# A two-layer encoder trunk on one core: how the MLPs' up products are placed, who adds the weight blocks, and when weights are loaded

## The chip, the cores and the metric

The kernel runs on one core of a Trainium2 chip. The metric is the device time of one execution in microseconds; the kernel before has a median of 1085.5 us over three runs (1084.59 to 1086.11).

## The reference

The input is 512 tokens of width 1024, float32. Two layers, each a token mixer and an MLP, with an RMSNorm ahead of each and residual adds:

```python
for layer in range(DEPTH):                       # DEPTH = 2
    hn = rmsnorm(h, norm_mix[layer])
    mix = chunked_band_attention(...) if layer == 0 else rglru_block(...)
    h = h + mix
    h = h + sq_relu_mlp(rmsnorm(h, norm_mlp[layer]), mlp_w1[layer], mlp_w2[layer])
return rmsnorm(h, norm_final)

def sq_relu_mlp(h, w1, w2):                      # w1: 1024 x 4096, w2: 4096 x 1024
    z = jax.nn.relu(h @ w1)
    return (z * z) @ w2
```

The change touches the two MLPs alone.

## The kernel before

**Split operands.** Each float32 operand is cast to a rounded part H (ScalarE, L156) and the rest L = raw − H (VectorE, L159), and each product is three matmuls, H·H, H·L and L·H (`mm3`, L253 to L256). So every weight tile of 128x1024 costs a ScalarE cast and a VectorE subtraction before TensorE can use it. `plan` lists the weight tiles in the order of their use; `want(n)` hands out the next n and lets `fetch` prepare tiles up to three ahead. The H and L buffers are five each (`wsp`), so a tile is cast when the buffer of the fifth before it is free.

**The MLP.** The hidden width of 4096 is cut into four parts p of 1024. The *up* products make the hidden values of a part, Relu and Square on ScalarE follow, and the *down* products of the part are added into the result tile `d`. Part 0's up products are eight plain tiles of 512 columns (`up`). All other products are done on blocks of a 2x2 partition with seven products in place of eight (Strassen–Winograd):

- An up *group* (p, g), with g = 0 or 1, makes half a part: seven *pieces* of 24 matmuls of 256 columns. Pieces use the weight tiles u11, us2, u12, us1, us3, us4, u22 in this order, and the activations hn or the sums r1 to r4. They accumulate in the PSUM banks b1, b6 and b5. Three partial results are kept: `c1`, a copy of b1 after the first piece (L777), `u` and `v`, VectorE sums of b6 and b5 with c1 (L782, L790). `out_` adds what is missing on VectorE (L769) and does Relu and Square (L771, L772).
- A down *round* p has seven *steps*, each 24 matmuls of 512 columns over two token tiles: weights 11, t1, 22, 21, t2, t3, t4 (two half tiles each) against the split hidden blocks 11, s1, s4, 12, s2, s3, 22. They accumulate in the PSUM bank pairs X and Y. After each step `read` (L723, VectorE) adds two banks into `d`, scaled by the norm's factor. `split` (L808, L809) splits the hidden blocks, `sums` and the subtraction at L850, L820, L821 and L816 form s1 to s4.

**Weight sums.** The block sums us1 to us4 and t1 to t4 are made by *adding transfers*: DMAs from the POOL queue with `accum_op=add`, onto a block in SBUF from HBM or from SBUF. us1 is the block 21 loaded into `kept` plus 22 (L124), us2 a second copy of 11 plus us1 (L125), us3 is 11 plus 21 (L170), us4 is 12 plus us2 (L172). Of a round's t blocks, t1 is 12 plus 11 from HBM (L116), t3 is 22 reloaded into 11's buffer plus 12 (L163, L164), t2 is 22 plus 12 (L166), t4 is 21 plus t2 (L168). SP's queue issues all plain loads; a group's loads are issued when its first tile is fetched (`upper`, L119 to L125), a round's when its tile 11 is fetched (`blocks`).

**Order.** In part 0's eight up products, `turn` moves the residual into `d`: 16 transposes on VectorE and 32 DMAs of 64 KB on SP (L716), and r1 to r4 are formed. In round p the first group of part p+1 is interleaved one piece behind each step; the second group of part p (for p > 0) runs before or within the opening of round p, five or six pieces in a row. Each engine runs its instructions in an order that the build fixes; it follows the order of the code where data and buffers are ready and moves ready instructions forward.

Of the kernel before, what the change touches and what calls it, by code (L numbers as in the profile page):

```python
# [40 lines left out]
def trunk(ctx: ExitStack, tc: tile.TileContext, xT, cols, gfin, win, wqkv, wo, rwin, rga, rgx, rwo, w1, w2, out):  # L41
# [59 lines left out]
    raws, start_ = {}, []  # L101

    def rows(src, h):
        return src[h * U : (h + 1) * U].rearrange("(k p) c -> p k c", p=P)
# [4 lines left out]
    def blocks(srcs):  # L109
        for name, src in srcs.items():  # L110
            both = state["raw"].tile([P, 2, 1024], F32, name=f"b{name}_{state['next']}", tag=f"b{name}")
            for h in range(2):
                raws[name, h] = both[:, h]
                nc.sync.dma_start(two(raws[name, h]), rows(src, h))
        for h in range(2):
            G.dma_start(two(raws["12", h]), rows(srcs["11"], h), accum_op=ALU.add)  # L116

    def upper(srcs):
        i = state["next"]  # L119
        for n, tag, src in (("11", "wr0", "11"), ("s1", 0, "21"), ("s2", "wr1", "11"), ("12", "wr2", "12"), ("22", 1, "22")):  # L120
            raws["u" + n] = state["kept"][:, tag] if n in ("s1", "22") else wraw.tile([P, 1024], F32, name=f"u{n}_{i}", tag=tag)
            nc.sync.dma_start(raws["u" + n].rearrange("p (k c) -> p k c", k=4), srcs[src].rearrange("(k p) c -> p k c", p=P))
        raws["us3"], raws["us4"] = raws["u11"], raws["u12"]
        G.dma_start(raws["us1"].rearrange("p (k c) -> p k c", k=4), srcs["22"].rearrange("(k p) c -> p k c", p=P), accum_op=ALU.add)  # L124
        G.dma_start(raws["us2"], raws["us1"], accum_op=ALU.add)  # L125

    def fetch():
        i = state["next"]
        kind, nk, srcs = plan[i]
        H = wsp.tile([P, 1024], F32R, name=f"wh{i}", tag="wh")  # L130
        L = wsp.tile([P, 1024], F32R, name=f"wl{i}", tag="wl")
        n = 1024
        if kind == "plain":
            n = nk * sum(src.shape[1] for src in srcs)
# [4 lines left out]
            for n_, src in enumerate(srcs):  # L139
                w = src.shape[1]  # L140
                queue = nc.scalar if i == 0 and n_ else nc.sync
                queue.dma_start(rv[:, :, c0 : c0 + w], src.rearrange("(k p) c -> p k c", p=P))
                c0 += w
        elif kind[0] == "u":
            nk = 4
            if kind == "u11":
                upper(srcs)
            raw = raws[kind]
        else:
            half, nk = nk, 2  # L150
            if kind == "11" and half == 0:
                blocks(srcs)
            raw = raws[{"t1": "12", "t2": "22", "t3": "11", "t4": "21"}.get(kind, kind), half]
        state["next"] += 1
# [7 lines left out]
        if kind == "11":  # L162
            nc.sync.dma_start(two(raw), rows(srcs["22"], half))  # L163
            G.dma_start(two(raw), rows(srcs["12"], half), accum_op=ALU.add)  # L164
        elif kind == "22":
            G.dma_start(raw, raws["12", half], accum_op=ALU.add)  # L166
        elif kind == "21":
            G.dma_start(raw, raws["22", half], accum_op=ALU.add)  # L168
        elif kind == "u11":
            G.dma_start(raw.rearrange("p (k c) -> p k c", k=4), srcs["21"].rearrange("(k p) c -> p k c", p=P), accum_op=ALU.add)  # L170
        elif kind == "u12":
            G.dma_start(raw, raws["us2"], accum_op=ALU.add)  # L172
# [31 lines left out]
    starts = []  # L204

    def add_mlp(layer):
        starts.append(len(plan))
        def up_(p, j):
            c0 = 2 * p * T + j * P
            plan.append(("plain", KT, [w1[layer][:, c0 : c0 + P]]))  # L210

        def add_group(p, g):
            c0 = (2 * p + g) * T
            srcs = {
# [3 lines left out]
            plan.extend(("u" + n, 4, srcs) for n in ("11", "s2", "12", "s1", "s3", "s4", "22"))  # L218

        for j in range(KT):  # L220
            up_(0, j)
        for p in range(4):
            srcs = {
# [3 lines left out]
            if p:  # L227
                add_group(p, 1)
            tail = [plan.pop()] if p == 3 else []
            if p < 3:  # L230
                add_group(p + 1, 0)
                tail = plan[-7:]
                del plan[-7:]
            for kind in ("11", "t1", "22", "21", "t2", "t3", "t4"):
                plan.extend((kind, half, srcs) for half in range(2))
                plan.extend(tail[:1])
                del tail[:1]
# [409 lines left out]
    def mlp(ly, norm):  # L647
        with ExitStack() as mctx:
# [23 lines left out]
            def right_split(n):  # L672
# [6 lines left out]
                if n == 4:  # L679
                    state["kept"] = per.tile([P, 2, 1024], F32, name=f"kept{ly}", tag="hx1")  # L680
# [47 lines left out]
            def up(p, j):  # L728
# [11 lines left out]
                if 1 <= j <= 2:  # L740
                    for k in range(4 * j - 4, 4 * j):
                        scaled(k)
                if 3 <= j <= 6:
                    for step_, n in (((right, 1), (right, 3)), ((right, 2), (right, 4), (right_split, 1)),
                                     ((right_split, 3),), ((right_split, 2), (right_split, 4)))[j - 3]:
                        step_(n)
# [10 lines left out]
            def group(p, g):  # L757
# [19 lines left out]
                S.copy(c1, b1)  # L777
# [11 lines left out]
                v = zp.tile([P, T], F32, name=f"v{ly}{p}{g}", tag="v")  # L789
                V.tensor_add(v, b5, c1)  # L790
# [8 lines left out]
                out_(1, 0, b6, c1, -1.0)  # L799
                yield  # L800

            def round_(p):
                low, raw = {}, {}
                raw["11"], raw["s1"] = a[p, 0, 0], a[p, 0, 1]

                def split(n, h):
                    H, L = zp.tile([P, 4, U], F32R, name=f"{h}{n}{ly}{p}", tag=h), take(F32R, f"l{n}{p}")
                    S.copy(H, raw[n])  # L808
                    V.tensor_sub(L, raw[n], f(H))  # L809
                    low[n] = (H, L)  # L810
                    give(raw[n])

                def sums(last):
                    if last:
                        raw["s4"] = take(F32, f"s4{p}")
                        V.scalar_tensor_tensor(raw["s4"], raw["12"], -1.0, raw["s2"], ALU.mult, ALU.subtract)  # L816
                    else:
                        raw["12"], raw["22"] = a[p, 1, 0], a[p, 1, 1]
                        raw["s2"] = take(F32, f"s2{p}")
                        V.tensor_sub(raw["s1"], raw["22"], raw["s1"])  # L820
# [39 lines left out]
                else:  # L860
# [3 lines left out]
                    for n in range(5):  # L864
                        next(here)
# [351 lines left out]
```

## Time and profile before

| what | value |
|---|---|
| median of 3 runs | 1085.5 us |
| profiled execution, its own time | 1087.62 us |
| its span (first to last instruction) | 1085.8 us |
| mean granted TensorE clock | 0.982 |
| TensorE busy | 1035.0 us, 95% |
| VectorE busy | 832.3 us, 77% |
| ScalarE busy | 638.5 us, 59% |
| first MLP: first up matmul to last down matmul | 244.7 us to 589.2 us |
| second MLP: first up matmul to the end of the span | 733.6 us to 1085.8 us |

Times inside the profile count from the start of the span. A row of the table of stretches gives, for a stretch of time, the busy time of each engine with its number of instructions, the granted clock of TensorE (1.00 is full), the busy share of the DMA engines (overlapping packets can carry it over 1) and GB/s. A row of the timeline gives start, length, engine, line, operation, `out<-in` by the program's tile names, and in brackets how long the engine stood idle before it and what ended that. Rows of waits give the total, the number and the longest.

### The profile page before, as it was taken

What the parts mean: (1) busy time and instruction counts of PE and PEld (TensorE: products, weight loads), DVE (VectorE), ACT (ScalarE), POOL (GpSimd) and SP (SyncE); (2) the same over time, 40 slices, a digit from 0 to 9 for tenths busy, and PEclk for the clock granted to TensorE, in tenths of its full rate; (3) what the DMA queues carried; (4) which work ended last, traced back from release to release, by engine and by line L of the source; (5) the groups of instructions that cost most, each with busy time, mean ns of one, the idle gap of its engine ahead of it and who ended that gap; (6) DMA issues with size and microseconds to landing.
All of it is one profiled execution on the core that took longest, in us unless ns stands there. A gap on an engine that the chain in (4) does not pass through costs nothing. (4 is left out here: it accounts for less than half of the span.)

```text
span 1085.8 us, 15138 instructions
## 1 busy us (share of the span) xinstructions
PE 1035.0 (95%) x5618; PEld 896.1 (83%) x5618; DVE 832.3 (77%) x1212; ACT 638.5 (59%) x984; POOL 129.1 (12%) x140
## 2 busy tenths in 40 slices
PE   9999999999959799999999999999959799999997
PEld 8788888888848798998978788888848798998976
DVE  7889778877458597787798998976447487697686
ACT  7667567457535465565567697556535365565565
POOL 1000000000121122122110000000221122121120
PEclk9999999999979999999999999999979899999999
DMA  8354253343979899999863313354969899999772
GB/s 272 99 145 127 59 175 97 93 150 89 284 135 277 216 193 247 274 198 261 242 117 101 113 59 97 96 175 118 290 108 274 219 184 236 282 202 254 184 152 78
DMA packets 149098, 189.27 MB, mean 174 GB/s; under 512 B 7585, under 2 KB 105889, under 8 KB 149025
## 3 DMA queue, kind: packets, MB, share of 16 engines
q1 hardware_dynamic: 119008, 128.87, 37.4%
q0 software_dynamic: 29440, 58.73, 31.2%
q8 instruction: 44, 0.72, 0.3%
q10 hardware_dynamic: 576, 0.72, 0.2%
q14 instruction: 30, 0.24, 0.1%
HBM read 148.43 MB, written 2.10 MB: 139 GB/s over the span
## 5 line engine op out<-in xcount | busy, mean ns | idle before, releaser
L156 ACT CAST wh<-b 128x1024 fp32r<-128x1024 f32 x112 | 117.0, 1049 | 77.9 <-PE m L255 53.1
L159 DVE TENSOR_TENSOR wl<-b,wh 128x1024 fp32r<-128x1024 f32 x112 | 135.7, 1221 | 16.1 <-ACT wh L156 16.0
L254 PE MATMUL m<-rH,wh 128*128 128x256 f32 x384 | 110.2, 287 | 22.4 <-ACT wh L156 22.4
L256 PE MATMUL m<-rH,wl 128*128 128x256 f32 x384 | 110.1, 287 | 2.3 <-DVE wl L159 2.3
L255 PE MATMUL m<-rL,wh 128*128 128x256 f32 x384 | 109.7, 286 | 0.0
L159 DVE TENSOR_TENSOR wl<-wr,wh 128x1024 fp32r<-128x1024 f32 (+1 forms) x74 | 87.7, 1189 | 17.5 <-ACT wh L156 17.0
L156 ACT CAST wh<-wr 128x1024 fp32r<-128x1024 f32 (+1 forms) x73 | 75.0, 1030 | 43.9 <-PE wo L255 11.8
L254 PEld LDWEIGHTS m<-rH,wh 128*128 128x128 f32 x384 | 74.8, 195 | 24.3 <-ACT wh L156 23.4
L254 PE MATMUL m<-hnH,wh 128*128 128x256 f32 x288 | 83.7, 291 | 11.6 <-ACT c L777 11.6
L159 DVE TENSOR_TENSOR wl<-u,wh 128x1024 fp32r<-128x1024 f32 x48 | 58.7, 1224 | 38.6 <-ACT wh L156 38.1
L255 PE MATMUL m<-hnL,wh 128*128 128x256 f32 x288 | 83.2, 289 | 0.0
L256 PE MATMUL m<-hnH,wl 128*128 128x256 f32 x288 | 83.1, 289 | 0.0
L156 ACT CAST wh<-u 128x1024 fp32r<-128x1024 f32 x48 | 50.4, 1049 | 53.1 <-PE x L256 19.3
L256 PEld LDWEIGHTS m<-rH,wl 128*128 128x128 f32 x384 | 74.7, 194 | 3.3 <-DVE wl L159 3.3
L255 PEld LDWEIGHTS m<-rL,wh 128*128 128x128 f32 x384 | 74.9, 195 | 0.9
L254 PEld LDWEIGHTS m<-hnH,wh 128*128 128x128 f32 x288 | 56.9, 198 | 13.1 <-ACT c L777 12.3
L116 POOL DMA_DIRECT2D b<-in_w x16 | 22.9, 1464 | 365.2 <-DMA b<-in_w 364.6
L159 DVE TENSOR_TENSOR wl<-us,wh 128x1024 fp32r<-128x1024 f32 x12 | 14.7, 1222 | 62.5 <-ACT wh L156 62.5
L255 PEld LDWEIGHTS m<-hnL,wh 128*128 128x128 f32 x288 | 56.9, 198 | 0.7
L256 PEld LDWEIGHTS m<-hnH,wl 128*128 128x128 f32 x288 | 56.9, 198 | 0.0
L156 ACT CAST wh<-us 128x1024 fp32r<-128x1024 f32 x12 | 12.6, 1046 | 73.1 <-DMA us<-kept 56.7
L256 PE MATMUL y<-wh,ls 128*128 128x512 f32 x128 | 50.2, 392 | 1.4 <-DVE ls L809 1.4
(383 smaller groups left out, 3077.1 us busy)
## 6 DMA issues: line engine op xcount, KB each, us to landing
b<-in_w SPq DMA_DIRECT2D x80, 512.0 KB, 8.1
b<-in_w POOLq DMA_DIRECT2D x32, 512.0 KB, 7.5
b<-b POOLq DMA_DIRECT2D x32, 512.0 KB, 7.0
u<-in_w SPq DMA_DIRECT2D x24, 512.0 KB, 10.0
kept<-in_w SPq DMA_DIRECT2D x24, 512.0 KB, 8.9
wr<-in_wqkv SPq DMA_DIRECT2D x20, 512.0 KB, 4.0
wr<-in_w SPq DMA_DIRECT2D x16, 512.0 KB, 4.2
wr<-in_rwin SPq DMA_DIRECT2D x16, 512.0 KB, 3.7
```

The lines of the kernel that those rows point to most:

```text
L116: G.dma_start(two(raws["12", h]), rows(srcs["11"], h), accum_op=ALU.add)
L156: S.copy(H[:, :n], raw[:, :n])
L159: low = V.tensor_sub(L[:, :n], raw[:, :n], f(H[:, :n]))
L254: PE.matmul(acc, WH, XH, start=start, stop=False, skip_group_check=more)
L255: PE.matmul(acc, WH, XL, start=False, stop=False, skip_group_check=more)
L256: PE.matmul(acc, WL, XH, start=False, stop=stop, skip_group_check=more)
```

## The change

**Order.** The eight up products of part 0 are traced ahead of round 0 (before, the last four stood inside it). In rounds 0 to 2 all 14 pieces of both groups of part p+1 are interleaved, two behind each step (behind the last step one, `sums`, one, `sums`). Round 3 has no pieces. `opening` and `sums` of the next round are done at the end of the round before it.

**Who adds weight blocks.** us2, us4 and both halves of t2 and t3 are now made on VectorE (an add or a subtraction of 128x1024 in SBUF, in `fetch`). us1, us3, t1 and t4 stay adding transfers; t1 and t4 add from SBUF. The second load of 11 in a group and the reload of 22 in a round go.

**Copies inside PSUM.** Where b1 was copied to `c1` and later added by VectorE, ScalarE copies b1 into b6, and piece r2 accumulates onto it (`piece(b6, "r2", False)`). `u` and `v` become ScalarE copies of b6 and b5. In a round X is copied into Y after step s4 and step 12 accumulates onto it; step 11 is no longer read.

**Loads.** A block is loaded as soon as its buffer's last use is fetched, one block at a time, for the group or round that follows; for the first ones the calls stand in `up` (j = 1, 3, 5) and behind the last plain tile.

```diff
+    def load_down(key, name): ...      # two SP loads of a block of the next round
+    def first_sum(key):
+        if key in down:
             for h in range(2):
-        for h in range(2):
-            G.dma_start(two(raws["12", h]), rows(srcs["11"], h), accum_op=ALU.add)
+                G.dma_start(raws["12", h], raws["11", h], accum_op=ALU.add)
+    def load_up(key, name):
...
+        raws["u" + name] = raw
+        nc.sync.dma_start(four(raw), rows(upper[key]["21" if name == "s1" else name]))
+        if name == "s1":
+            G.dma_start(four(raw), rows(upper[key]["22"]), accum_op=ALU.add)
...
             nk = 4
-            if kind == "u11":
-                upper(srcs)
+            following = (key[0], key[1] + 1)
+            if kind == "us2":
+                raws["us2"] = wraw.tile([P, 1024], F32, name=f"us2_{key[0]}{key[1]}", tag=f"wr{(state['base'] + 2) % 3}")
+                V.tensor_add(raws["us2"], raws["u11"], raws["us1"])
+                raws["us3"] = raws["u11"]
+                G.dma_start(four(raws["us3"]), rows(upper[key]["21"]), accum_op=ALU.add)
+            if kind == "us4":
+                raws["us4"] = raws["u12"]
+                V.tensor_add(raws["us4"], raws["us4"], raws["us2"])
             raw = raws[kind]
...
+            if kind == "t2":
+                V.tensor_add(raw, raw, raws["12", half])
+                G.dma_start(raws["21", half], raw, accum_op=ALU.add)
+            if kind == "t3":
+                V.tensor_sub(raw, raws["22", half], raw)
...
+        if kind == "plain_":
+            state["base"] = state["plain"] % 3
+            load_up((nk_layer[i], 0), "11")
+            load_up((nk_layer[i], 0), "12")
+        elif kind == "us1":
+            load_up(following, "s1")
+        elif kind == "us3":
+            load_up(following, "11")
+        elif kind == "us4":
+            load_up(following, "12")
+        elif kind == "u22":
+            load_up(following, "22")
+        elif kind == "t2" and half:
+            load_down(following, "12")
+        elif kind == "t3" and half:
+            load_down(following, "11")
+            first_sum(following)
+        elif kind == "t4" and half:
+            load_down(following, "22")
+            load_down(following, "21")
...
+            ups = [("u" + n, 4, (layer, 2 * p + g)) for g in range(2) for n in ("11", "s2", "12", "s1", "s3", "s4", "22")]
+            for n, kind in enumerate(("11", "t1", "22", "21", "t2", "t3", "t4")):
+                plan.extend((kind, half, (layer, p)) for half in range(2))
+                if p < 3:
+                    plan.extend(ups[2 * n : 2 * n + 2])
...
-                b1 = mmp(f"m1{ly}{p}{g}")
+                b1, b6 = mmp(f"m1{ly}{p}{g}"), mmp(f"m6{ly}{p}{g}")
                 piece(b1, "11", True)
-                c1 = wk.tile([P, T], F32, name=f"c1{ly}{p}{g}", tag="nsq", bufs=2)
-                S.copy(c1, b1)
+                S.copy(b6, b1)
                 yield
-                b6 = mmp(f"m6{ly}{p}{g}")
-                piece(b6, "r2", True)
+                piece(b6, "r2", False)
                 u = wk.tile([P, T], F32, name=f"u{ly}{p}{g}", tag="nsq", bufs=2)
-                V.tensor_add(u, b6, c1)
+                S.copy(u, b6)
...
-                V.tensor_add(v, b5, c1)
+                S.copy(v, b5)
...
-                out_(1, 0, b6, c1, -1.0)
+                out_(1, 0, b6, None, -1.0)
...
-                        read(bank[t], t0 + t, c)
+                        if name != "11":
+                            read(bank[t], t0 + t, c)
+                        if name == "s4":
+                            S.copy(Y[t], X[t])
...
+                ups = (x for g in range(2) for x in group(p + 1, g)) if p < 3 else iter(range(14))
+                def rise(n):
+                    for _ in range(n):
+                        next(ups)
+                step("11", X, True, 0, 0)
+                rise(2)
+                split("s4", p)
                 step("s1", Y, True, 2, 1)
-                next(then)
-                split("12", "h0")
+                rise(2)
+                split("12", p)
                 step("s4", Y, False, 0, 1)
-                next(then)
-                split("s2", "h1")
-                step("12", Y, True, 0, 0)
+                rise(2)
+                split("s2", p)
+                step("12", Y, False, 0, 0)
...
                 step("s3", X, False, 2, 1)
-                next(then)
+                opening(p + 1)
+                rise(2)
                 step("22", X, False, 2, 0)
-                next(then)
+                rise(1)
+                sums(p + 1, False)
+                rise(1)
+                sums(p + 1, True)
...
-            for j in range(4):
+            for j in range(KT):
                 up(0, j)
+            sums(0, False)
+            sums(0, True)
```

More of the change, by code (lines that the diff above doesn't have):

```diff
@@ L118, in upper, with four @@
[L118 to L125, printed above, removed]
+    def four(t):
+        return t.rearrange("p (k c) -> p k c", k=4)
@@ new lines, in rows, with load_down @@
+    def rows(src):
+        return src.rearrange("(k p) c -> p k c", p=P)
+    def load_down(key, name):
+        if key not in down:
+            return
+        both = state["raw"].tile([P, 2, 1024], F32, name=f"b{name}_{key[0]}{key[1]}", tag=f"b{name}")
+        for h in range(2):
+            raws[name, h] = both[:, h]
+            nc.sync.dma_start(two(raws[name, h]), rows(down[key][name][h * U : (h + 1) * U]))
+    def first_sum(key):
+        if key in down:
+            for h in range(2):
+                G.dma_start(raws["12", h], raws["11", h], accum_op=ALU.add)
@@ L798, in group @@
                 piece(b6, "r4", False)
-                out_(1, 0, b6, c1, -1.0)
+                out_(1, 0, b6, None, -1.0)
                 yield
-            def round_(p):
[L803 to L820, printed above, removed]
-                        V.scalar_tensor_tensor(raw["s2"], raw["22"], -1.0, raw["s3"], ALU.mult, ALU.subtract)
+            low, raw, turn_ = {}, {}, [0]
```

167 lines of the change are left out of this document (74 added, 93 removed).

## The prediction

> **What bounds the kernel now.** I read the page first, then the list of waits of TensorE, then one table of stretches, and the timeline only inside the stretches where TensorE stood still.
>
> ```profile
> span 1085.8 us, 15138 instructions
> ...
> DMA  8354253343979899999863313354969899999772
> ...
> q1 hardware_dynamic: 119008, 128.87, 37.4%
> q0 software_dynamic: 29440, 58.73, 31.2%
> ```
>
> ```profile
> PE m L254 <- ACT wh L156: 22.4, 2, 12.2
> PE m L254 <- ACT c L777: 11.6, 3, 5.2
> PE m L256 <- DVE wl L159: 2.3, 4, 0.8
> ```
>
> ```profile
> 245.00:285.00 40.00, 40.00 (x178) 33.10 (x177) 24.05 (x33) 28.37 (x62) 2.60 (x2) 1.00 0.55 143
> 357.60:363.60 6.00, 6.00 (x48) 5.77 (x47) 0.00 (x0) 0.46 (x1) 1.08 (x1) 1.00 1.13 247
> 302.40:320.00 17.60, 4.96 (x26) 4.51 (x26) 5.29 (x6) 5.79 (x6) 3.95 (x4) 0.61 0.53 93
> 364.50:377.00 12.50, 6.75 (x42) 6.34 (x41) 11.37 (x23) 8.47 (x12) 2.20 (x2) 0.86 0.60 153
> 390.00:550.00 160.00, 160.00 (x1015) 145.49 (x1014) 126.49 (x130) 94.06 (x109) 32.13 (x30) 1.00 0.98 230
> 556.50:560.50 4.00, 2.56 (x10) 1.50 (x9) 3.44 (x5) 3.60 (x4) 1.29 (x2) 1.00 0.99 189
> 790.90:809.00 18.10, 6.26 (x27) 5.56 (x27) 7.08 (x7) 8.19 (x9) 4.79 (x5) 0.62 0.44 75
> 853.40:868.50 15.10, 9.13 (x51) 8.72 (x52) 11.89 (x12) 9.09 (x12) 2.21 (x2) 0.77 0.66 174
> 880.00:1000.00 120.00, 120.00 (x745) 108.42 (x744) 97.30 (x101) 69.98 (x80) 26.66 (x25) 1.00 1.01 226
> 1048.00:1052.00 4.00, 2.55 (x10) 1.51 (x9) 3.44 (x5) 3.65 (x4) 0.86 (x1) 1.00 1.02 198
> ```
>
> The columns of the table are the length, busy time of PE, PEld, DVE, ACT and POOL with their instructions, granted clock, DMA share and GB/s. In the long stretches (390 to 550, 880 to 1000) TensorE is busy throughout at clock 1.00: nothing can be won there. The first two rows give its pace: 40 us for 178 matmuls of 512 columns is 0.225 us each, 6 us for 48 of 256 columns about 0.12. A down step or an up product has 24 of them, 5.4 and 2.9 us; a round of 7 steps and 14 products is 7 × 11.2 = 78 us. What is left to win are the short rows, in which TensorE stands and then runs at a lower clock. DMA is at 0.98 to 1.01 in the full stretches: the transfers only just keep up, and where the up groups begin they don't.
>
> ```profile
> 249.62 20.62 SPq L716 DMA_DIRECT2D d<-turned  x32
> ...
> 284.59 0.53 SPq L122 DMA_DIRECT2D kept<-in_w  x1
> ...
> 298.21 1.31 POOL L124 DMA_DIRECT2D kept<-in_w  x1 [6.68 <-issue]
> ...
> 305.94 1.47 POOL L125 DMA_DIRECT2D us<-kept  x1
> 313.63 1.04 ACT L156 CAST wh<-us 128x1024 fp32r<-128x1024 f32 x1 [13.98 <-DMA us<-kept]
> ...
> 314.73 0.58 PE L254 MATMUL m<-rH,wh 128*128 128x256 f32 x1 [12.18 <-ACT wh L156]
> ```
>
> This is the whole of the first stall: a load at 284.59, its adding transfer 13.6 us later, a second adding transfer onto `us` 7.7 us after that, 7.7 us more until the cast. Three transfers in series make the second up product late by 12.2 us.
>
> **What the change removes.** Stalls, each as length less work at the pace above. 302.4 to 320.0: 17.6 − 24 × 0.12 = 14.7. 790.9 to 809.0: 18.1 − (24 × 0.12 + 2 × 0.225) = 14.8. 364.5 to 377.0: 12.5 − 42 × 0.12 = 7.5. 853.4 to 868.5: 15.1 − 51 × 0.12 = 9.0. These are 46.0 us. The third transfer is gone (`us2` is a VectorE add), the products run two by two from the first round on, so none stands seven in a row as around 360, and the loads no longer saturate: adding transfers fall from 112 (8 rounds with 8, 12 groups with 4) to 56 (4 and 2), and SP's weight loads of the MLPs from 140 (10 and 5) to 112 (8 and 4), 84 × 0.524 MB less. At the share per MB of the two queue rows (0.29% and 0.53%) that is 28 × 0.524 × 0.29 + 56 × 0.524 × 0.53 = 20 points of the span; the MLP stretches are about half of it, so their DMA share goes from 1.0 to about 0.6. In the last round the split of `s4` has one step more of room than before: the rows 556.5 and 1048 lose their idle 1.44 and 1.45, 2.9 us. Removed: **48.9 us**.
>
> **When the first `us2` is ready.** Its load moves behind the 32 `turned` transfers on SP, which end at 270.2, and eight weight loads queued beside it, so to some 272.5 in place of 284.59. With the same 13.6 + 1.3 + 7.7 us it is summed at 295, added (1.23) and cast (1.04) at 297.4. TensorE wants it when the first step (from 288.2), one product and the hand-off below are through: 288.2 + 5.4 + 2.9 + 0.8 = 297.3. In the second MLP the same counts leave about 2 us of room. Bounds: 0 if the loads are faster without the saturation, 8 us for both if they wait as long as today's worst; nearest is the row just used, I take **2 us**. What waits there: VectorE behind its add (splits of `s1`, later weights), ScalarE behind the cast, TensorE behind both.
>
> ```profile
> 289.77 1.23 DVE L820 TENSOR_TENSOR a<-a,a 128x1024 f32<-128x1024 f32 x1 [6.21 <-ACT a L737]
> ...
> 299.13 1.41 DVE L723 SCALAR_TENSOR_TENSOR d<-x,rq,d 128x512 f32<-128x512 f32 x2
> ...
> 345.24 0.69 DVE L769 TENSOR_TENSOR a<-m,v 128x512 f32<-128x512 f32 x1 [0.56 <-PE m L256]
> ...
> 372.94 0.58 ACT L777 COPY c<-m 128x512 f32<-128x512 f32 x1
> ...
> 373.57 0.58 PE L254 MATMUL m<-hnH,wh 128*128 128x256 f32 x1 [5.18 <-ACT c L777]
> ...
> L255 PE MATMUL m<-rL,wh 128*128 128x256 f32 x384 | 109.7, 286 | 0.0
> ```
>
> **VectorE.** A round gains 8 adds of 128x1024 at 1.23 us (`us2` and `us4` of two groups, two halves each of `t2` and `t3`), 9.8 us, and loses two reads (1.4) and six adds out of PSUM (4.1): +4.3 us of 78. It is at 126.49 of 160 and 97.30 of 120 now, 79 to 81%; it goes to about 86%. Beside TensorE that costs nothing: a tile is cast when a buffer of five comes free, four tiles (11 us) ahead. Without that cover it would be all 8 adds, 59 us over six rounds. The last round is all down: 14 weight splits, 4 adds and 6 splits of `a` at 1.23 and 12 reads at 0.70 are 37.9 us beside TensorE's 38. Bounds 0 (the lead carries it) to 2 × 4 × 1.23 = 9.8 us; I take **2 us**, since the four adds come in a row and the lead is more than twice as long.
>
> **ScalarE.** Four copies more per group pair (`u`, `v`) and two of Y from X: 6 × 0.58 = 3.5 us a round, on an engine at 94.06 of 160. The Y copy waits for a read behind `s4`: 1.4 + 0.6 us under two products of 2.9; in the last round 0.7 + 0.6 under the other half of the step, 2.7. The copy from b1 to b6 is not covered in the first group of each round: products `11` and `r2` stand next to each other, and `r2` accumulates onto the copy. TensorE waits for the end of its last matmul (286 ns long, 0.12 apart: 0.16), ScalarE's start (0.05, taken as TensorE's own: 372.94 + 0.58 to 373.57), the copy, 0.05: 0.84 us, six times, **5.0 us**. No row copies into PSUM; bounds are the copies out of it (0.58) and a copy queued behind one cast (1.04 more), so 5 to 11 us; I take the row, since ScalarE mostly waits for TensorE. In the second group a whole down step lies between.
>
> The page ScalarE: Activation LUTs of the Trainium skill (section on the step-by-step stages) says that ScalarE reaches PSUM faster than SBUF. No row here shows it; by it the six hand-offs would cost somewhat under 5 us, by the row 5.0.
>
> **The sum**, against the profiled execution's own 1087.6: 1087.6 − 48.9 + 2 + 2 + 5.0 = 1047.7. That execution was 2.1 us above the median of the runs (1085.5), so **1045.6 us**. With the three added terms at their bounds it is 1041.6 to 1045.6 + 6 + 7.8 + 6 = 1065; waits of TensorE too short for the table, some 4 us in all that may go too, carry the low end to 1037.
>
> **Rivals.** *The first stalls stay.* The `turned` transfers still hold SP to 270.2 and the loads behind them are more at once than before. For it: 13.6 us from load to adding transfer although SP was free. Against: 12 us earlier, one transfer less in series. One stall kept whole, less the 1 us in the sum: 1045.6 + 14 = 1059; both: 1073. *The short waits pull the clock down.* The rows 302.4 to 320 and 364.5 to 377 show it after a stall (0.61, 0.86); 14% of 12.5 us below full is 3.5 us at half speed, 1.75 us lost. Six times: 1056. Against: rows 556.5 and 1048, 1.4 us idle at clock 1.00. The Trainium skill warns of this on TensorE: Matmul & The Clock Gate, section on psum-queue depth-cycling: short idles between groups of matmuls can make the clock swing. By that rule 1056, by the two rows 1045.6. *No gain*: the stalls return in equal size because the remaining `us1` chain decides, 1085. *Slower*: the adds stand in VectorE's order, ahead of reads and weight splits, and each can wait for an adding transfer or a late predecessor; ScalarE's cast then waits for VectorE, which waits for ScalarE in turn. A round has about 11 us of VectorE to spare; with x us of waiting at each of 8 adds six rounds lose 6 × (8x − 11). Slower than before from x = 2.2; at x = 2.5 it is 1045.6 + 54 = 1100. For it: VectorE at 86%. Against: every addend is loaded five tiles (14 us) or more ahead, and in the full stretches now, with 80% and DMA at 1.0, TensorE never waits.
>
> **How the numbers follow.** Forecast 0.65; first stalls stay 0.13; clock 0.07; no gain 0.04; slower 0.11. What reaches from 1037 to 1072 holds most of the first three, about 0.8; the likeliest case alone is 1037 to 1060. A difference of 0.2% (2.2 us) is about what a measurement of this kernel can tell. Faster 0.85, same 0.04, slower 0.11.
>
> **What would show it.** Right: no idle stretch over 3 us of TensorE in either MLP and a granted clock of 1.00 there; DMA share near 0.6 in the rounds; six waits of TensorE for ScalarE's copy, under 1 us each; VectorE near 86%. Wrong: a wait of 5 us or more before the first `r2`, TensorE waiting for weight splits in the middle of a round, or a lowered clock behind each copy. The forecast falls if VectorE is at 100% in the rounds.

## The result and the profile after

The changed kernel takes 1075.8 us (median of 12 runs, 1071.08 to 1080.76), the kernel before 1085.13 (12 runs, 1083.42 to 1086.48): ratio 0.9917, interval [0.99, 0.9933]. It is faster by 0.8%, about 9 us, where 40 were forecast, and 3.8 us above the range. The profiled execution of the changed kernel took 1071.1 us, 4.7 below its own median.

From the page of the kernel after (busy time of the engines, DMA share in 40 slices, the queue of the adding transfers):

```profile
PE 1032.4 (97%) x5618; PEld 893.5 (84%) x5618; DVE 858.5 (80%) x1216; ACT 658.5 (62%) x1024; POOL 68.1 (6%) x84
...
DMA  8354253253857837738613413163847837738413
...
q0 software_dynamic: 17280, 29.36, 16.2%
```

Where the DMA row had its 9s in the two MLPs it has 3 to 8 now, and the adding queue went from 58.73 to 29.36 MB. The table of stretches of the kernel after, columns as in the prediction:

```profile
282.20:291.10 8.90, 3.72 (x10) 2.37 (x9) 3.32 (x3) 5.16 (x8) 0.00 (x0) 0.81 1.02 288
303.20:306.50 3.30, 2.28 (x11) 1.45 (x10) 3.30 (x4) 3.30 (x5) 0.00 (x0) 1.00 0.64 102
310.00:380.00 70.00, 70.00 (x446) 63.75 (x445) 60.29 (x88) 41.33 (x52) 8.73 (x8) 1.00 0.70 175
384.50:393.40 8.90, 5.16 (x28) 4.65 (x27) 5.54 (x5) 4.57 (x6) 0.00 (x0) 0.81 0.20 60
394.00:466.00 72.00, 72.00 (x462) 65.70 (x461) 57.63 (x57) 43.28 (x53) 8.74 (x8) 1.00 0.69 169
468.40:475.30 6.90, 3.43 (x16) 3.04 (x15) 5.25 (x5) 3.81 (x5) 0.00 (x0) 0.75 0.05 11
476.00:548.00 72.00, 72.00 (x458) 65.50 (x457) 59.06 (x58) 45.10 (x55) 6.11 (x6) 1.00 0.58 150
548.00:588.00 40.00, 39.31 (x190) 32.28 (x189) 39.08 (x45) 28.24 (x43) 1.74 (x2) 1.00 0.32 79
766.30:772.40 6.10, 3.61 (x10) 2.35 (x9) 3.24 (x3) 4.32 (x8) 0.00 (x0) 0.72 1.00 312
866.00:870.00 4.00, 0.93 (x6) 0.51 (x6) 3.97 (x5) 3.44 (x5) 0.00 (x0) 1.00 0.00 0
947.70:956.70 9.00, 5.05 (x28) 4.63 (x27) 5.81 (x5) 4.41 (x6) 0.00 (x0) 0.81 0.20 58
```

The long rows are as forecast: TensorE busy throughout, clock 1.00, DMA 0.58 to 0.70. The four stalls of before (302, 364, 791, 853) are gone, and seven short rows have come. Taken like the stalls of the prediction, as length less work at 0.225 or 0.12 us a matmul, they fall into two kinds:

- **Beginnings of the MLPs** (282, 303, 766): 6.65 + 0.8 + 3.85 = 11.3 us.
- **First groups of later rounds** (384, 468, 866, 948): 5.1 + 5.0 + 3.3 + 5.2 = 18.6 us.

The waits of TensorE after (releaser, total us, number, longest) put names to them: the row with `m L809` is the second kind, the row `u` the larger part of the first (282 and 766). Of the row `wl` one wait is that at 303; the other, 1.2 us at 785, is in none of the seven short rows. The row `d` (1.4 us) stands in the last rounds.

```profile
PE m L274 <- ACT m L809: 14.2, 4, 4.0
PE u L274 <- ACT wh L178: 7.7, 2, 5.2
PE y L275 <- DVE wl L181: 2.2, 2, 1.2
PE y L274 <- DVE d L741: 1.4, 2, 0.7
```

The copy's 18.6 are 14.2 of waiting and 4.4 more, which go with the lowered clock that follows (0.81, 0.75, 0.81 in three of the four rows). With the last rounds' 1.4 us it all comes to 31.3 us, where the sum had 2 + 2 + 5.0 = 9. That makes 1047.7 + 22.3 = 1070.0 for an execution that took 1071.1, and the wait at 785 is about the difference. The sum's frame holds; the copy's term is too small, and a term for the last plain tile is missing.

**The copy.** ScalarE's timeline in the kernel after, at the first group of round 1:

```profile
384.23 1.05 ACT L839 CAST hs<-s 128x1024 fp32r<-128x1024 f32 x1 [1.59 <-DVE s L854]
385.19 1.03 ACT L178 CAST wh<-u 128x1024 fp32r<-128x1024 f32 x1
386.13 1.04 ACT L839 CAST h<-a 128x1024 fp32r<-128x1024 f32 x1
387.08 1.04 ACT L178 CAST wh<-kept 128x1024 fp32r<-128x1024 f32 x1
388.03 0.57 ACT L809 COPY m<-m 128x512 f32<-128x512 f32 x1
```

And TensorE's around it:

```profile
383.02 0.28 PE L276 MATMUL m<-hnH,wl 128*128 128x256 f32 x1
...
384.52 0.39 PE L274 MATMUL y<-wh,hs 128*128 128x512 f32 x1
388.65 0.39 PE L274 MATMUL m<-rH,wh 128*128 128x256 f32 x1 [3.74 <-ACT m L809]
```

Piece 11 issues its last matmul at 383.02. The copy of its bank could follow at once; it stands behind four casts, the first of which waits for VectorE's `s4`, and begins at 388.03. TensorE has seven matmuls of step s1 as cover (383.14 to 384.52) and then waits. In the prediction's words it is "a copy queued behind one cast"; here it is four.

**The beginning.** SP's queue in the kernel after, and then ScalarE's cast of the last plain tile:

```profile
249.24 20.61 SPq L734 DMA_DIRECT2D d<-turned  x32
269.90 2.46 SPq L118 DMA_DIRECT2D b<-in_w  x4
272.44 0.50 SPq L154 DMA_DIRECT2D wr<-in_w  x1
273.00 8.05 SPq L134 DMA_DIRECT2D u<-in_w  x2
```

```profile
286.70 1.04 ACT L178 CAST wh<-wr 128x1024 fp32r<-128x1024 f32 x1 [2.78 <-DMA wr<-in_w]
```

The tile is issued at 272.44 behind four weight loads of the first round, shares saturated DMA (1.02 in the row at 282) with them and those behind it, and is cast 14.3 us later. Before, it was issued at 270.67, ahead of those loads, and cast at 278.13. TensorE has nothing else to do: the eighth up product is the last plain one, and the weights of step 11, which follows, are cast behind this tile in ScalarE's order (at 287.65).

### The profile page after: what moved, and what is told of

The parts are those of the page before. It is cut to its first block, busy times and chain, and to the rows that moved or that the text cites. A ratio compares the mean times of both kernels' runs of the same rounds, so it can differ in the third digit from the quotient of the medians.

```text
span 1069.3 us, 14950 instructions
## 1 busy us (share of the span) xinstructions
PE 1032.4 (97%) x5618; PEld 893.5 (84%) x5618; DVE 858.5 (80%) x1216; ACT 658.5 (62%) x1024; POOL 68.1 (6%) x84
## 3 DMA queue, kind: packets, MB, share of 16 engines
q1 hardware_dynamic: 108320, 114.18, 34.6%
q0 software_dynamic: 17280, 29.36, 16.2%
## 4 chain that ended last, share of the span: by engine, by line
PE 45%; DVE 13%; DMA 6%; issue 4%; ACT 3%; SPq 1%; DVEq 0%; ACTq 0%; POOLq 0%
PE m L274 6%; PE m L275 6%; PE m L276 6%; DMA kept<-in_w 5%; DVE wl L181 5%; PE y L275 4%; PE y L276 4%; PE y L274 4%; PE x L274 2%; PE x L275 2%; PE x L276 2%; ACT wh L178 2%; PE ro L275 1%; PE ro L274 1%; PE ro L276 1%
## 5 line engine op out<-in xcount | busy, mean ns | idle before, releaser
L274 PE MATMUL m<-rH,wh 128*128 128x256 f32 x384 | 110.6, 288 | 14.2 <-ACT m L809 14.2
L274 PE MATMUL m<-hnH,wh 128*128 128x256 f32 x288 | 81.4, 283 | 0.0
L274 PE MATMUL u<-hnH,wh 128*128 128x512 f32 x128 | 51.2, 400 | 7.7 <-ACT wh L178 7.7
L274 PE MATMUL x<-wh,h 128*128 128x512 f32 (+1 forms) x132 | 51.7, 394 | 1.3 <-DVE d L1015 1.3
L275 PE MATMUL y<-wl,hs 128*128 128x512 f32 x128 | 50.5, 395 | 2.2 <-DVE wl L181 2.2
L274 PE MATMUL y<-wh,hs 128*128 128x512 f32 x128 | 50.2, 392 | 1.4 <-DVE d L741 1.4
```

What stands on the lines that cost most here:

```text
L274: PE.matmul(acc, WH, XH, start=start, stop=False, skip_group_check=more)
L275: PE.matmul(acc, WH, XL, start=False, stop=False, skip_group_check=more)
```

## The experiments

All kernels compute the whole reference. Their times are medians of four runs, each ratio is to the kernel before on the same chip. "After" is the changed kernel.

**1. The copy ahead of the casts.** An edge in the build's order keeps every cast that the code has behind the copy behind it on ScalarE. Nothing else is changed.

```diff
+    def behind(ins):
+        if state.get("copy"):
+            after(ins, state["copy"])
...
-            S.copy(H[:, :n], raw[:, :n])
+            behind(S.copy(H[:, :n], raw[:, :n]))
...
-                S.copy(b6, b1)
+                state["copy"] = S.copy(b6, b1)
...
-                S.copy(H, raw[n])
+                behind(S.copy(H, raw[n]))
```

> The changed kernel with ScalarE's copy of b1 into b6 forced ahead of every cast traced behind it (an ordering edge on ScalarE alone; no work is added or removed). Theory A, the copy stands too late in ScalarE's order: the four waits of TensorE for it in rounds 1 and 2 (3.9, 3.6, 3.2 and 4.1 us, 19.5 us with the lowered clock behind them) shrink to under 1 us each, and the time falls by 14 to 18 us, to about 1060. Theory B, VectorE forms the sums s1, s2 and s4 too late at the round's start and the copy only shows it: TensorE then waits as long for the split of s4 one step on, and the time stays within 4 us of 1076.

Measured 1058.07 us, 0.9752 [0.9726, 0.9779]: 17.7 us less than after, as theory A has it and close to the 18.6 of the four rows. Its first two waits of TensorE:

```profile
PE u L278 <- ACT wh L182: 5.7, 1, 5.7
PE m L278 <- DVE a L806: 3.7, 2, 2.1
```

The wait for the copy (14.2 us after) is gone from the whole list; of the beginnings' `u` waits that of the first MLP stays, and in the second MLP waits in step s1 have taken its place. So the copy's place in ScalarE's order cost what the table shows, and the copy itself next to nothing.

**2. The last plain tile's load ahead of the first round's.** The loads of 12, 22 and 21 are moved behind it and behind the first group's.

```diff
                 if j == 1:
...
                     load_down((ly, 0), "11")
-                    load_down((ly, 0), "12")
-                    first_sum((ly, 0))
...
                 if j == 3:
...
-                    load_down((ly, 0), "22")
-                    load_down((ly, 0), "21")
                 if j == 4:
...
                     opening(0)
+                    load_down((ly, 0), "12")
+                    first_sum((ly, 0))
                 if j == 5:
...
                     load_up((ly, 0), "22")
+                    load_down((ly, 0), "22")
+                    load_down((ly, 0), "21")
```

> The changed kernel with the first round's loads of blocks 12, 22 and 21 put behind the last plain up tile's load and behind the first group's loads. Theory C, the last plain tile is late because four 512 KB loads stand ahead of it on SP behind the turned transfers: the waits of 5.3 and 2.7 us before the eighth up product go (11.2 us with the lowered clock), time about 1065. Rival C2, the transfers are saturated there (DMA share 1.0) and whatever comes last is late: the wait moves to the first us2 or to t1, and the time stays within 4 us of 1076.

Measured 1069.81 us, 0.9859 [0.9839, 0.988]: 6.0 less, where 11 were at stake, between the two expectations. Its first two waits of TensorE:

```profile
PE m L274 <- ACT m L809: 16.5, 5, 4.3
PE y L274 <- ACT hs L839: 2.4, 1, 2.4
```

The `u` wait is gone, but waits in step s1 (`y`), for its split and for a weight tile's cast, have come in its place: what is loaded next is late instead. Going by the time, the order of the loads was about half of what the beginnings lose.

**3. Both together.** Edits 1 and 2 in one kernel.

> Both edits together. A and C: the gains add up, 25 to 29 us, time about 1048, and the granted clock stays at 1.00 through both MLPs but for the end. B or C2: less than half of that.

Measured 1052.29 us, 0.9695 [0.9674, 0.9716]. That is 23.5 us less than after; 17.7 + 6.0 = 23.7, so here the two gains add, within intervals of 4 to 6 us, and the copy and the last plain tile's load can be taken as two causes. It is less than the 25 to 29 us that were expected: losses of 4.5 and 5.3 us in step s1 are left at the two beginnings.

**4. The old partial sums.** The changed kernel with `c1`, `u` and `v` as before: the copy goes to SBUF, r2 starts afresh, VectorE adds.

```diff
-                S.copy(b6, b1)
+                c1 = wk.tile([P, T], F32, name=f"c1{ly}{p}{g}", tag="nsq", bufs=2)
+                S.copy(c1, b1)
...
-                piece(b6, "r2", False)
+                piece(b6, "r2", True)
...
-                S.copy(u, b6)
+                V.tensor_add(u, b6, c1)
...
-                S.copy(v, b5)
+                V.tensor_add(v, b5, c1)
...
-                out_(1, 0, b6, None, -1.0)
+                out_(1, 0, b6, c1, -1.0)
```

> The changed kernel with the group's partial results kept as before the change: c1 copied to SBUF, u and v made and added by VectorE, r2 into a fresh bank. TensorE no longer needs the copy before r2. Theory A: the four waits go as in e1, while VectorE has 4 us more per round (busy near 90%), time 1058 to 1064. Theory B: VectorE is later still at each round's start, time 1076 or more.

Measured 1053.34 us, 0.971 [0.9678, 0.9743]: theory A's direction, 5 us below its range, and far from theory B. TensorE no longer waits for ScalarE's copy at all, and the adds given back to VectorE show as short waits for `v`. From its waits of TensorE:

```profile
PE m L274 <- DVE v L822: 2.2, 2, 1.5
```

Moving a group's partial sums into PSUM (the copy of X into Y in a round stays here) thus costs 22 us (1075.8 to 1053.3) as it was built. Experiment 1, with the copy in its place, is within 5 us of this.

**5 and 6. The first group's loads ahead of the first round's.** Experiments 4 and 1, each with the loads in the order of the last plain tile, s1, 11, 12, 22 of the first group, then 12, 22, 21 of the first round.

```diff
...
-            load_up((nk_layer[i], 0), "11")
-            load_up((nk_layer[i], 0), "12")
...
-                    load_down((ly, 0), "12")
-                    first_sum((ly, 0))
...
-                    load_down((ly, 0), "22")
-                    load_down((ly, 0), "21")
...
-                    load_up((ly, 0), "s1")
-                    load_up((ly, 0), "22")
+                    for name in ("s1", "11", "12", "22"):
+                        load_up((ly, 0), name)
+                    load_down((ly, 0), "12")
+                    first_sum((ly, 0))
+                    load_down((ly, 0), "22")
+                    load_down((ly, 0), "21")
```

> The partial results kept as before the change, and the first group's loads put right behind the last plain tile's: block 21 for us1 first, then 11, 12 and 22, and only then the first round's 12, 22 and 21. Theory D, the waits that are left at each MLP's start come from the order in which SP issues loads into saturated transfers: the wait for the eighth plain tile (about 7 and 5 us with the clock) goes, us1 is summed before it is wanted, and the time falls 9 to 12 us below the 1053.3 of the kernel with old partials alone, to about 1043. Rival D2, the transfers are the bound there and some block is late in any order: 1048 to 1053.

> The changed kernel with the copy of b1 forced ahead in ScalarE's order and the same new order of the first loads. Theory D: the 4.5 and 5.3 us before the first down step s1, which the kernel with both edits still had because VectorE's us2 add waited for us1, fall to under 1 us each; time 1052.3 - 8 = about 1044. Rival D2: 1050 to 1053.

Measured 1054.75 us, 0.9723 [0.9699, 0.9746], and 1057.35 us, 0.9745 [0.9722, 0.9769]: nothing gained over 4 and 1. Theory D falls; both lie above even the rival's range, and experiment 6 is 5 us behind experiment 3, which has the other order. In experiment 5 VectorE's `us2` add moved from 297.69 (after) to 288.39, as wanted, but the round's `t1` is late now. POOL's queue there:

```profile
290.25 1.32 POOL L163 DMA_DIRECT2D u<-in_w  x1 [11.60 <-DVE us L161]
291.04 2.33 POOL L123 DMA_DIRECT2D b<-b  x2
```

The adding transfer of `t1` (`b<-b`) stands behind that of `us3`, which waits for VectorE's `us2`; `t1` is cast at 298.64. Experiment 6 loses 8.0 and 9.75 us in step s1. In each of the orders tried, some tile of the first round is late. That too much has to be moved in that time is likely, with a DMA share of 0.86 from 270 to 295 and 0.97 from 280 to 290 in experiment 6, but not shown apart from POOL's order, which holds `t1` back as well.

**7. us2 and us4 by adding transfers again.** Experiment 6, with the second load of 11 and the two transfers of the kernel before in place of VectorE's adds.

```diff
+        if name == "11":
+            raws["us2"] = wraw.tile(...)
+            nc.sync.dma_start(four(raws["us2"]), rows(upper[key]["11"]))
+            G.dma_start(raws["us2"], raws["us1"], accum_op=ALU.add)
...
-                V.tensor_add(raws["us2"], raws["u11"], raws["us1"])
...
-                V.tensor_add(raws["us4"], raws["us4"], raws["us2"])
...
+        elif kind == "u12":
+            G.dma_start(raw, raws["us2"], accum_op=ALU.add)
```

> As the kernel with the copy first and the new order, but us2 and us4 are made by adding transfers again, us2 with its second load of block 11 (24 adds of VectorE gone, 24 adding transfers and 12 loads more). Theory E, three transfers in series were what made the first up products late: the wait before the first r2 returns with 5 to 12 us and a lowered clock in each MLP, time 1055 to 1070. Rival E2, the early issue alone covers the third transfer: within 3 us of the kernel with the copy first and the new order, or below it, since VectorE has less to do.

Measured 1069.93 us, 0.9862 [0.9827, 0.9897], 12.6 over experiment 6. The time lies at the top of theory E's range, but not for its reason: the first stall is the same (8.2 us), and the loss is at the starts of later rounds (6.3, 3.7 and 4.0 us). TensorE's first wait, and ScalarE's timeline at round 1:

```profile
PE y L279 <- ACT hs L844: 13.0, 4, 5.4
```

```profile
380.68 1.05 ACT L183 CAST wh<-us 128x1024 fp32r<-128x1024 f32 x1 [10.26 <-DMA us<-kept]
```

The cast of `us2` waits for its transfer. In ScalarE's order Relu and Square of the hidden values stand behind it (381.64 and 382.29), VectorE's sum s1 needs them (382.96), and the split `hs` needs the sum (384.22). So the adds on VectorE are worth 12 us where ScalarE's order would otherwise wait for a transfer. At the first beginning they show no gain: there `t1` is the late tile in both kernels (cast at 298.96 and 300.03).

**8. Experiments 4 and 2 together.**

> The partial results kept as before the change, and the first round's loads of 12, 22 and 21 behind the last plain tile's and the first group's (the order that gave 6 us before). If the two gains add up, the 7.5 and part of the 4.6 us at the start of each MLP go and the time is 1053.3 - 6 = about 1047; if the first loads are bound by the transfers in any order, 1051 to 1054.

Measured 1052.25 us, 0.9693 [0.9661, 0.9726]. That is 1 us less than experiment 4, within the intervals: here the two gains do not add. The first beginning now loses 2.2 us, but 3.8 and 5.1 us are lost later (362 and 833), where a piece waits for VectorE's `v`, and `v` is queued behind the `us2` add, which waits for us1 (`kept`).

**9 and 10. The `turned` transfers on two queues.** What all of these share is that SP's queue issues 32 transfers of 64 KB until 270 and only then the weight loads. Here POOL issues those of the second token half: experiment 9 is 8 with it, experiment 10 is 3 with it.

```diff
-                            nc.sync.dma_start(
+                            (G if h else nc.sync).dma_start(
```

> As the kernel with old partials and the last plain tile first, with the 16 turned transfers of the second token half issued by POOL in place of SP (nothing else moves). Theory F, SP is held by the 32 turned transfers until 270 us and the first loads start too late: they start some 10 us earlier, the waits at each MLP's start fall under 2 us, time 4 to 8 us below the kernel it is built on. Rival F2, the transfers are saturated from then on and an earlier issue only queues them: within 2 us of it.

> As the kernel with the copy first and the last plain tile first (1052.3), with the same 16 transfers on POOL. F: the 4.5 and 5.3 us before the first step s1 go, time 1043 to 1046, which is the sum of the forecast. F2: 1051 to 1053.

Measured **1038.34** us, 0.9567 [0.9545, 0.959], and **1040.0** us (1039.86 to 1040.79), 0.958 [0.9565, 0.9594]. They beat the kernel before and the changed one, and their intervals overlap. Both go further down than theory F gave (4 to 8 us below experiment 8, and 1043 to 1046). SP's queue in experiment 10, then POOL's, the busy times from its page and its waits of TensorE:

```profile
249.74 12.28 SPq L738 DMA_DIRECT2D d<-turned  x16
262.13 0.52 SPq L158 DMA_DIRECT2D wr<-in_w  x1
```

```profile
250.90 8.71 POOL L738 DMA_DIRECT2D d<-turned  x16 [82.32 <-ACT h L686]
```

```profile
PE 1024.4 (99%) x5618; PEld 888.7 (86%) x5618; DVE 855.5 (82%) x1216; ACT 657.2 (63%) x1024; POOL 86.0 (8%) x116
```

```profile
PE y L278 <- DVE d L745: 1.4, 2, 0.7
PE m L278 <- DVE a L806: 1.3, 1, 1.3
```

The last plain tile's load is issued at 262.13 in place of 272.44, and in experiment 10 no kind of wait comes to more than 1.4 us. One moved queue was worth 12.3 us over experiment 3 and 13.9 over experiment 8, more than the beginnings had left to give in experiment 3 (4.5 + 5.3): small waits went with them. Of experiment 9 remain waits for `v`. VectorE's timeline there:

```profile
438.81 1.23 DVE L161 TENSOR_TENSOR us<-u,kept 128x1024 f32<-128x1024 f32 x1 [9.61 <-DMA kept<-in_w]
...
441.09 0.68 DVE L822 TENSOR_TENSOR v<-m,c 128x512 f32<-128x512 f32 x1
```

VectorE waits 9.61 us for us1's adding transfer, and the read `v` comes behind it. This is what the copies on ScalarE are good for: they don't stand in that order. Experiments 9 and 10 trade one short wait for another and end level, so with the loads early enough the partial sums in PSUM bring no gain that could be measured.

**11. VectorE's adds alone.** The kernel before, with only us2 and us4 made on VectorE. No other part of the change; us3's adding transfer moves behind the us2 add, which still reads block 11.

```diff
-        for n, tag, src in (("11", "wr0", "11"), ("s1", 0, "21"), ("s2", "wr1", "11"), ("12", "wr2", "12"), ("22", 1, "22")):
+        for n, tag, src in (("11", "wr0", "11"), ("s1", 0, "21"), ("12", "wr2", "12"), ("22", 1, "22")):
...
-        G.dma_start(raws["us2"], raws["us1"], accum_op=ALU.add)
...
+            if kind == "us2":
+                raws["us2"] = wraw.tile([P, 1024], F32, name=f"us2_{i}", tag="wr1")
+                V.tensor_add(raws["us2"], raws["u11"], raws["us1"])
+                G.dma_start(raws["u11"].rearrange("p (k c) -> p k c", k=4), srcs["21"].rearrange("(k p) c -> p k c", p=P), accum_op=ALU.add)
+            if kind == "us4":
+                V.tensor_add(raws["us4"], raws["us4"], raws["us2"])
...
```

> The kernel before with one part of the change alone: us2 and us4 added by VectorE in place of the adding transfers and the second load of 11; order, loads and partial results as before. If three transfers in series made the stalls, each of the four falls by one transfer, 7 to 8 us: the second ones (7.5 and 9.0) nearly go, the first ones halve, time 1055 to 1065. If the late issue of the loads made them, they stay within 4 us of the kernel before.

Measured 1107.51 us, 1.0204 [1.0184, 1.0223]: 21 us slower, and neither expected time holds. The first stall of each MLP does halve, as expected (from 14.7 and 14.8 us to about 7 and 8, at 302 and 793), but six new waits of TensorE cost more than that. Its first wait of TensorE, and VectorE's timeline at one of the six:

```profile
PE x L255 <- DVE d L724: 37.9, 6, 8.0
```

```profile
838.98 1.23 DVE L149 TENSOR_TENSOR us<-u,kept 128x1024 f32<-128x1024 f32 x1 [10.45 <-DMA u<-in_w]
...
841.26 1.41 DVE L724 SCALAR_TENSOR_TENSOR d<-x,nrq,d 128x512 f32<-128x512 f32 x2
```

VectorE stands 10.45 us before an add whose block is still in flight; the reads of X are queued behind it, and TensorE waits for them. That is the prediction's "slower" rival, on the kernel before. In the changed kernel the blocks are loaded earlier, and its waits of TensorE have no such row: these adds need the early loads. Which of the loads and the interleaving of the products does it is not separated.

**12. Two queues alone.** The changed kernel with the edit of 9 and nothing else.

> The changed kernel with the 16 turned transfers of the second token half on POOL and nothing else. Theory F: the waits at the start of each MLP go (7.0 + 1.5 and 4.2 + 1.7 us in the profile of the changed kernel, with the lowered clock), the four waits for ScalarE's copy stay, time 1075.8 - 14 = about 1062. If the two causes are not independent, so that the copy's lateness in rounds 1 and 2 comes from the late start, it falls to 1050 or less.

Measured 1068.41 us, 0.9843 [0.9826, 0.9859], 7.4 less than after, about half of the 14 that theory F gave. Its first two waits of TensorE:

```profile
PE m L274 <- ACT m L809: 15.0, 5, 4.3
PE y L274 <- ACT hs L839: 3.4, 1, 3.4
```

The copy's wait stays, so the late start is not what makes the copy late. The second MLP's beginning is mended; the first loses 9.5 us (295.7 to 309.2) in step s1. Experiment 10, which has the order of experiment 2 and the copy first as well, loses nothing there; which of the two does it, no run separates.

## Why the prediction was right and wrong

**The removed stalls: right in size, the reason shown in part.** The rows at 302, 364, 791 and 853 are gone, rounds run at full pace and clock 1.00. DMA is at 0.58 to 0.70 where "about 0.6" was forecast; the 20 points of the span were right within 3 (37.4 + 31.2 before, 34.6 + 16.2 after), but by the two rows of the table at the start the MLPs are 64% of the span and not "about half", which would have given 0.7. Of the reasons that the prediction names, one transfer less in series halves the first stalls (experiment 11) and does not remove them; with the early loads, the first beginning loses no more with all three transfers than without the third (experiment 7). What the interleaving of the products is worth alone, no run shows. The sum itself is reached once the two wrong terms are mended: without the 2 us of the beginning and with 0.7 us of copy waits, all that is left of them in experiment 3, the forecast would be 1045.6 − 2 − 4.3 = 1039.3; experiment 10 measured 1040.0. So close a match is in part luck, since experiment 10 keeps short waits of other kinds and its interval is 3 us wide.

**The copy: the step that failed most.** The prediction took 5.0 us for six hand-offs of 0.84 us, with the reason that "ScalarE mostly waits for TensorE", and bounded it by "a copy queued behind one cast". It measured 18.6 us at four places. The average load of ScalarE (62%) said nothing about this place: the splits of s4 and of block 12 and two weight casts are due just there, and the build's order put all four, the first of them waiting for VectorE, ahead of the copy. With the copy ahead (experiment 1) it costs less than forecast, since the build lays matmuls of s1 between pieces 11 and r2, which the prediction said stand next to each other.

The prediction's own lines had the sign. In the kernel before, TensorE waits 5.18 us at 373.57 for the copy that starts at 372.94, although piece 11 issued its last matmul at 364.42. In ScalarE's order three weight casts (365.29 to 367.18) stood ahead of the copy, and then Relu, which waited 2.44 us for VectorE, Square and a split:

```profile
370.67 0.63 ACT L771 ACTIVATE a<-a 128x512 f32<-128x512 f32 x1 [2.44 <-DVE a L769]
...
371.99 1.04 ACT L808 CAST h<-a 128x1024 fp32r<-128x1024 f32 x1
```

The prediction took the copy's length and its hand-off from this place and counted the wait among the stalls that go. There a whole piece, r2, lay between piece 11 and the product that needed the copy; the change lets r2 itself need it.

**The beginning: a term that was left out.** The prediction costed only `us2` (2 us). That part came out: the add came at 297.69, 2.6 us later than in the working (297.4 less the add and the cast, 295.1), and the two waits for `wl`, which VectorE makes behind it, are 2.2 us. What it put at nothing is the last *plain* tile, for which TensorE stood still ahead of that: 10.5 of the 11.3 us (rows 282 and 766). The working counted the "eight weight loads queued beside it" as time of SP's queue, not as bytes that share the DMA engines with the tile in front. Its rival "the first stalls stay" named the right resource, the `turned` transfers that hold SP to 270 and loads that are more at once (experiments 9, 10 and 12), though not the tile and not the size.

**VectorE: right.** It is at 80 to 86% in the long stretches (60.29 of 70, 57.63 of 72) and at 39.08 of 40 in the last round, at the price of two waits of 0.7 us where 2 us were taken.

**The clock: right price, wrong occasion.** The rival put 1.75 us on each of six waits of 0.84 us. The waits of that length that came lowered no clock (0.7 us in the row at 548 and 1.0 us in the row at 303, both at 1.00). The copy's waits of 3 to 4 us did in three cases of four, and the 4.4 us lost beside the waiting are 1.5 us for each of the three. The rule of the Trainium skill on TensorE: Matmul & The Clock Gate, section on psum-queue depth-cycling, that short idles between groups of matmuls can make the clock swing, is not seen here at the hand-offs' length. In experiment 10 the mean granted clock is 0.999.

**ScalarE into PSUM: no difference.** The page ScalarE: Activation LUTs of the Trainium skill (section on the step-by-step stages) would have the copy inside PSUM shorter than the one to SBUF. The tile views (lowest, median and longest ns, first and last start) show 578 ns after and 579 ns before:

```profile
L809 ACT COPY m<-m x12: 571/578/586, 305.6 to 989.7; 128x512 f32<-128x512 f32 x12
```

```profile
L777 ACT COPY c<-m x12: 572/579/582, 299.1 to 1022.9; 128x512 f32<-128x512 f32 x12
```

**No gain and slower: not here.** The "slower" rival was no empty threat: experiment 11 shows it at +21 us in the kernel before, where the loads aren't early. Of the signs that the prediction gave for being wrong, two came: a wait of 5.2 us ahead of the first r2, and the lowered clock behind three of the four copies.

In numbers, the 30.2 us between forecast and median are 22.3 for the copy, the beginnings and the last rounds, 1.1 left over in the profiled execution, 4.7 by which that execution lies below its median, and 2.1 by which the one of before lay above its own.

**Open.** Why executions of the changed kernel are spread over 10 us while the four of experiment 10 lie within 1. The granted clock goes along with it: it is 0.990 in the execution of 1071.08 us and 0.981 in that of 1080.76, and 0.9% of the time is the whole spread. What decides whether a stall brings a stretch of lower clock, no run here separates. And why the split queue mends waits in later rounds too (362 and 833 in experiment 8) isn't worked out.

## What to carry to other kernels

Before an operation on an in-order engine is costed at its own duration, read in its timeline what will be due on that engine at that moment and what those instructions wait for; the mean load doesn't tell. When loads are moved earlier, add up the bytes in flight around the tile that is needed first, since it shares the DMA engines with all that stand beside it. And where many small transfers hold a queue, look for a second queue beside another order of the loads: here the queue was worth 7 us alone and 12 to 14 on top of the other edits, the order 6 at most.

## What the runs showed of the hardware

- **Issuing many transfers holds a queue.** SP takes 20.61 us to issue 32 transfers of 64 KB and 12.28 for 16, POOL 8.71 for 16. Split over both they are out 8 us earlier.
- **Short idles and the clock.** The length of an idle alone doesn't decide. In the row at 866 TensorE stands 3.07 of 4 us and the clock stays at 1.00, from 870 to 880 too; in experiment 8 a stretch with 2.02 us idle (7.20 less 5.18 us) is at 0.76:

```profile
362.00:369.20 7.20, 5.18 (x29) 4.79 (x29) 6.47 (x17) 2.54 (x4) 0.00 (x0) 0.76 0.47 141
```

- **An add onto SBUF by transfer takes more of the DMA engines than a load.** Before, the adding queue took 31.2% of the DMA engines for 58.73 MB, the plain one 37.4% for 128.87 MB: 0.53 against 0.29 points per MB.
